# Value projections with 512-wide weights, an earlier split of one weight block, and a copy moved to ScalarE, in a kernel of two transformer blocks

## The chip, the cores and the metric

The kernel runs on one core of a Trainium2 chip. The metric is the device time of one execution in microseconds (us); the median of several executions is compared. All data is float32; many matmuls read a 32-bit format (fp32r) that TensorE streams faster, and each exact product is made of three such matmuls: a weight and an activation are each split into an upper and a lower part, and upper x upper, upper x lower and lower x upper are added up in PSUM.

## The reference

256 tokens of width 1024 pass through two blocks, each with one layer. Cut to what the change touches:

```python
def first_block(x, ...):
    h = rmsnorm(x, g_mix)
    z = h @ w_in                      # columns: pool 512, q 1024, k 1024, v 1024
    v = z[..., 2560:].reshape(B, S, 8, 128)
    y_attn = diff_attention(q, k, v, ...)
    ...                               # pooling branch, gates, output projection, FFN
def second_block(x, ctx, ...):
    hx = modulate(rmsnorm_2(x, ...), sh1, sc1)
    hc = modulate(rmsnorm_2(ctx, ...), csh1, csc1)
    ... nk_c, nv_c = hc @ w_in[kv columns]       # keys and values of 256 context tokens
    ... nq, nk, nv = hx @ w_in                   # queries, keys, values of the tokens
    o_mla = mla_latent_attention(...)
    o_na = neighbourhood_attention(nq, nk, nv, nk_c, nv_c, na_rel_bias)   # 8 heads of 64
    ...                               # output projection, 16 experts in 4 groups, final norm
```

## The kernel before, in words

The program is written for the Tile framework: the Python code emits instructions, Tile allots the buffers, adds the waits and orders the instructions of each engine by priority and by when it reckons them ready. A further dependency without a semaphore can be put between two instructions of one engine with `order(later, earlier)` (line 149); it only fixes their order.

Weights come as blocks of 1 MB, 128 partitions x 2048 columns. `load` (line 179) issues the DMA on the SP queue into one of four raw buffers `w`. `split_block` (line 212) calls `split` (line 188) for each half: ScalarE casts 1024 columns to the upper part (line 192) and VectorE subtracts it for the lower part (line 193), into one of four buffers `whl`. So a block takes two of four, and the next but one block waits for TensorE to be through with it. `mm3` (line 221) issues the three matmuls of one product. `dense_steps` (line 238, matmuls in lines 249 to 251) makes 256 output columns for 256 tokens; its weights are the stationary operand.

In the first block, a planner (`Jobs`, line 93) interleaves generators by rank, with an estimated TensorE cost and a latency at each `yield`. The generators are `feed` (line 710), `stats` (line 490) and two `head_lane`s. `feed` emits two pool blocks (tile upool), then for each pair p of four pairs of heads the query block and the key block (`qk_block`) and the value block (`v_block`), and then eight gate blocks. From the third pair on it waits until both heads of the pair two before are through. `stats` emits the mean of squares of x: `squares` on ScalarE and VectorE (lines 357 to 363, sums in tile sqa), four small matmuls into tile ms (line 369), then on VectorE mse (line 498) and epsq (line 499), then the reciprocal root: logarithm and exponential on ScalarE (tile ry), three operations on VectorE (lines 336 to 338, result rcol). A head waits for its values with `when(("v", p))` (line 677) ahead of the product with the probabilities (tile pv).

The value block is the other way round than `dense_steps`: the activations are stationary and the weights stream. In `v_block` (line 540) each of four blocks streams 256 columns of weights; one PSUM bank holds both halves of the tokens:

```python
for tb in range(2):
    for k in range(8):
        hi, lo = w(k, 256)
        mm3(ps[:, tb * 256:(tb + 1) * 256], (xh[...], xl[...]), (hi, lo), k == 0, k == 7)
```

`scaled_split` (line 318) then empties each half: ScalarE writes vh (line 320), VectorE vl (line 321). Banks 0 and 1 rotate in this stage through `mmbank`: query, value and gate blocks each take the next one; so before, all query blocks were on one bank and all value blocks on the other. Key blocks have bank 2.

In the second block, `feed2` (line 1275) emits the values of the neighbourhood attention (`na_values`, line 954, tile nav) for the context (activations ch, cl) and then for the tokens (hxh, hxl); between them stands the latent projection of the context (`kv_lat`, tile kvl, which has weights of its own, split aside). Both weight blocks are split ahead. The tokens' activations are made meanwhile by `modulated` (line 832). Then come four `na_pair`s (line 981), each with keys (tile nak) and queries (tile naq). Each query, scaled by 0.125, is stored as upper and lower part, twice, on partitions 0 to 63 and 64 to 127, by lines 998 to 1001 in tile napair. The softmax of two lanes of heads follows on VectorE and ScalarE (`softmax_pv`, line 1010: maximum in line 1026, its negation nm in lines 1022 and 1028, exponential in line 1029, transposes tp, casts ph and pl).

The experts come last: 16 experts in turns of four gate and up blocks (tile gu) and two down blocks (tile y), 96 weight blocks of 1 MB through a ring of 17 buffers (`eload`, line 1353, issued in line 1356); a load is issued when its ring buffer is free. TensorE's products there are in line 1754.

Of the kernel before, what the change touches and what calls it, by code (L numbers as in the profile page):

```python
# [15 lines left out]
OP = mybir.AluOpType  # L16
# [6 lines left out]
EPS = 1e-6  # L23
# [34 lines left out]
NAVP = 100  # L58

MM = 0.328  # L60
# [61 lines left out]
def tile_two_blocks(ctx, tc, a):  # L122
    nc = tc.nc
# [17 lines left out]
    def mmbank(name):  # L141
        b = mm_banks[0]
        mm_i[0] += 1
        return bank(b[mm_i[0] % len(b)], name)
# [34 lines left out]
    def load(ap, shape=(128, 2048), slot=None):  # L179
        if slot is None:  # L180
            w = wraw.tile(list(shape), F32, name="w", tag="w")
        else:
            w = big(slot, list(shape), F32, "w")
        with tc.high_priority(offset=0):
            nc.sync.dma_start(w, ap)
        return w

    def split(src, n):
        t = whl.tile([128, 2048], F32R, name="whl", tag="w")
        hi, lo = t[:, 0:n], t[:, 1024:1024 + n]  # L190
        with tc.high_priority(offset=AHEAD_SPLIT):
            nc.scalar.copy(hi, src)  # L192
            nc.vector.tensor_sub(lo, src, hi)  # L193
        return hi, lo

    def split_fine(w):

# [14 lines left out]
    def split_block(w):  # L212
        parts = [split(w[:, i * 1024:(i + 1) * 1024], 1024) for i in range(2)]

        def at(idx, width):
            o = idx * width
            g, r = divmod(o, 1024)
            return parts[g][0][:, r:r + width], parts[g][1][:, r:r + width]
        return at

    def mm3(out, w, x, start, stop):
        i = matmul(out, w[0], x[0], start=start, stop=False).ins
        matmul(out, w[0], x[1], start=False, stop=False)
        matmul(out, w[1], x[0], start=False, stop=stop)
        return i
# [92 lines left out]
    def scaled_split(hi, lo, src, gain):  # L318

        nc.scalar.activation(hi, src, AF.Copy, scale=gain)  # L320
        nc.vector.scalar_tensor_tensor(lo, src, gain, hi, op0=OP.mult, op1=OP.subtract)
# [162 lines left out]
    done = set()  # L484
# [5 lines left out]
    def stats():  # L490

        with low_priority(SQP):
            acc = squares(xT)
        use_table("natural_log_exp_and_others")
        yield 0, LAT_ST
        ms = bank(7, "ms")
        mean_mm(ms, acc)
        nc.vector.tensor_scalar(mse, ms[:, :2], EPS, None, op0=OP.add)
        nc.vector.tensor_scalar(epsq, mse, EPS, None, op0=OP.mult)
        rstd(rcol, mse, 2)  # L500
        yield 0.43, 2.0
        rb_ps = bank(7, "rb_ps")
        rows_of_cols(rb_ps, rcol)
        nc.vector.tensor_copy(rb, rb_ps[:, :T])
        small_inputs()
        yield 0.86, 0.5, when("u")
        for b in range(2):
            nc.vector.tensor_mul(upad[:, 2 * b:2 * b + 2, 16:], ups[b].rearrange("p (m t) -> p m t", m=2),
                                 rb.unsqueeze(1).to_broadcast([128, 2, T]))
        wg = big(11, [128, 2, 512], F32R, "wg")  # L510
        wgh, wgl = wg[:, 0], wg[:, 1]
        copy_split(wgh, wgl, load(a["w_grp"], (128, 512)))
        for g in range(4):
            yield 0, LAT_POOL
            pool_group(g, wgh, wgl)
            yield 0.35
# [22 lines left out]

    def v_block(b):  # L540

        w = split_block(load(a["w_in"][10 + b]))
        ps = mmbank("v")
        for tb in range(2):
            for k in range(8):
                hi, lo = w(k, 256)
                mm3(ps[:, tb * 256:(tb + 1) * 256],
                    (xh[:, k, tb * 128:(tb + 1) * 128], xl[:, k, tb * 128:(tb + 1) * 128]), (hi, lo),
                    k == 0, k == 7)
                yield MM  # L550
        for tb in range(2):
            scaled_split(vh[:, tb, b * 256:(b + 1) * 256], vl[:, tb, b * 256:(b + 1) * 256],
                         ps[:, tb * 256:(tb + 1) * 256], rcol[:, tb:tb + 1])
        done.add(("v", b))

    def gate_block(g):
        half, j = divmod(g, 4)
# [152 lines left out]
    def feed():  # L710
        for b in range(2):
            ups.append(bank(3 + b, "upool"))
            if b == 0:
                yield from dense_steps(ups[b], split_fine(first), xs, groups=[range(i, i + 2) for i in range(0, 8, 2)])
            else:
                yield from dense_steps(ups[b], split_block(load(a["w_in"][b])), xs)
        done.add("u")
        for p in range(4):
            if p >= 2:
                yield 0, 0, lambda: pair[p - 2]["heads"] == 2  # L720
            yield from qk_block(p, 0)
            yield from qk_block(p, 1)
            yield from v_block(p)
            for i in MODQ[p]:
                mod_block(i, MODS.get(i))
        for n, g in enumerate((0, 4, 1, 5, 2, 6, 3, 7)):
            yield from gate_block(g)
            for i in MODG[n]:
                mod_block(i, MODS.get(i))
# [215 lines left out]
    def value_split(t, kb, heads, src):  # L945

        hi, lo = (t[:, kb, heads, n, :] for n in range(2))
        s = src.rearrange("p (h e) -> p h e", e=64)
        copy_split(hi, lo, s)
# [2 lines left out]
    nav = [value_tile(7), value_tile(8)]  # L952

    def na_values():
        wv = [split_block(load(a["w_in2"][4 + b])) for b in range(2)]
        yield
        for n in range(2):
            if n == 1:
                yield "context"
                yield 0, 3.0, when("hx")  # L960
            for b in range(2):
                ps = mmbank("nav")
                for tb in range(2):
                    for k in range(8):
                        mm3(ps[:, tb * 256:(tb + 1) * 256],
                            (srcs[n][0][:, k, tb * 128:(tb + 1) * 128], srcs[n][1][:, k, tb * 128:(tb + 1) * 128]),
                            wv[b](k, 256), k == 0, k == 7)
                        yield MM
                for tb in range(2):
                  with tc.high_priority(offset=NAVP):  # L970
                    value_split(nav[n], tb, slice(4 * b, 4 * b + 4), ps[:, tb * 256:(tb + 1) * 256])

    def proj(ps, w, c0, n, kt=8, width=256, x=None, koff=0):

# [6 lines left out]
    def na_pair(p):  # L981
        w = split_block(load(a["w_in2"][p]))
        nb = load(a["na_bias"][p])
        t = big((3, 6)[p % 2], [128, 2048], F32R, "napair")
        psk = mmbank("nak")
        for n in range(2):
            yield from proj(psk[:, n * 256:(n + 1) * 256], w, 0, n)

        rows = slice(0, 64), slice(64, 128)
        keys = t[:, 0:512], t[:, 512:1024]  # L990
        for j in range(2):
            nc.scalar.copy(keys[j][rows[j]], psk[rows[j]])
            nc.vector.tensor_sub(keys[j][rows[1 - j]], psk[rows[j]], keys[j][rows[j]])
        psq = mmbank("naq")[:, :T]
        yield from proj(psq, w, 128, 1)
        qh, ql = (t[:, 1024:1280], t[:, 1280:1536]), (t[:, 1536:1792], t[:, 1792:2048])
        for j in range(2):
            nc.scalar.activation(qh[j][rows[j]], psq[rows[j]], AF.Copy, scale=0.125)
            nc.vector.scalar_tensor_tensor(ql[j][rows[j]], psq[rows[j]], 0.125, qh[j][rows[j]], op0=OP.mult, op1=OP.subtract)
            nc.scalar.activation(qh[j][rows[1 - j]], psq[rows[j]], AF.Copy, scale=0.125)  # L1000
            nc.vector.scalar_tensor_tensor(ql[j][rows[1 - j]], psq[rows[j]], 0.125, qh[j][rows[j]], op0=OP.mult,
                                           op1=OP.subtract)
        J.add(0, ready(("na", p), 1.2))
        pair["na", p] = qh, ql, keys, nb

# [936 lines left out]
def blocks(w, width):  # L1942
    K, M = w.shape
    return np.ascontiguousarray(
        w.reshape(K // 128, 128, M // width, width).transpose(2, 1, 0, 3).reshape(M // width, 128, -1))


def layout(i):
# [9 lines left out]
    o["cols"] = np.ascontiguousarray(np.concatenate([cols_of(p) for p in parts], axis=1))  # L1958
    o["lambda_qk"] = i["lambda_qk"].reshape(1, 256)
    o["w_in"] = blocks(i["w_in"][0], 256)  # L1960
    o["w_gate"] = blocks(i["w_gate"][0], 256)
    o["w_grp"] = np.ascontiguousarray(i["w_pool_grp"][0].transpose(1, 0, 2).reshape(128, 512))
    o["w_bp"] = blocks(i["w_branch_pool"][0], 512)
# [20 lines left out]
    o["b_mod"] = np.ascontiguousarray(i["b_mod_2"][0].reshape(6, D))  # L1984
    w = i["w_in_2"][0]
    q_lat, na_q, kv_lat, kr, na_k, na_v = np.split(w, np.cumsum([384, 512, 256, 32, 512]), axis=1)
    sw = np.concatenate([kr[:, 16:], kr[:, :16]], axis=1)
    pairs = [p for m in range(4) for p in (na_k[:, m * 128:(m + 1) * 128], na_q[:, m * 128:(m + 1) * 128])]
    o["w_in2"] = blocks(np.concatenate(pairs + [na_v, kv_lat, kr, sw, kr, sw, q_lat[:, 256:], q_lat[:, :256]],
# [63 lines left out]
```

## Time and profile before

| | us |
|---|---|
| median of 3 runs | 875.27 |
| lowest and highest | 875.26, 877.39 |
| the profiled execution | 877.89 |
| its span, first to last instruction | 876.1 |
| TensorE (PE) busy in it | 850.8 |
| VectorE (DVE) busy | 559.7 |
| ScalarE (ACT) busy | 425.9 |

The median is that of executions without the profiler; the profile is of one execution. A row of the order of time has a start, a duration, the engine, the line, the operation and the tiles written and read. Matmuls are pipelined: a row's duration is a modelled one and longer than the distance to the next start, so the cost of a matmul in a queue is read from the starts.

### The profile page before, as it was taken

To read this page: it belongs to the slowest core of one execution; us is meant where nothing else is said; L and a number is where in the kernel's file an instruction comes from. 1 tells how busy PE (TensorE), PEld (TensorE's weight loads), DVE (VectorE), ACT (ScalarE), POOL (GpSimd) and SP (SyncE) were. 2 spreads that over 40 slices of the span, in tenths; PEclk is the share of its full clock that TensorE was granted. 3 is DMA by queue.
4 is the path that set the end of the run, shared out by engine and by line. 5 is a ranking of instruction groups with operands and counts; after the bars stand their busy time and mean duration, and the time that the engine had idled before them with its cause. 6 is when DMAs were issued, how large, how long until landed. Compare 5 with 4: busy or idle time off the path is not lost. (4 is left out here: it accounts for less than half of the span.)

```text
span 876.1 us, 14580 instructions
## 1 busy us (share of the span) xinstructions
PE 850.8 (97%) x5827; PEld 691.9 (79%) x5827; DVE 559.7 (64%) x1137; ACT 425.9 (49%) x800; POOL 15.4 (2%) x28
## 2 busy tenths in 40 slices
PE   8999999999999999999999999999989999999995
PEld 7998999999999999999999988889943333334331
DVE  6898778799988768777855899997741111111104
ACT  6487787744564555546754687797520000000002
POOL 1000000000000000000000000000001000001001
PEclk9999999999999999999999999999899999999998
DMA  7762555577887665768524225546879999999970
GB/s 278 276 246 97 183 177 198 205 266 272 316 300 266 232 251 203 282 206 303 190 78 144 97 79 186 191 144 237 335 263 416 426 427 427 426 426 427 425 315 33
DMA packets 34781, 224.51 MB, mean 256 GB/s; under 512 B 4479, under 2 KB 6143, under 8 KB 8458
## 3 DMA queue, kind: packets, MB, share of 16 engines
q1 hardware_dynamic: 31256, 216.18, 65.3%
q10 hardware_dynamic: 2674, 5.16, 1.6%
q0 software_dynamic: 768, 2.10, 0.6%
q8 instruction: 49, 0.80, 0.4%
q14 instruction: 34, 0.28, 0.1%
HBM read 220.53 MB, written 3.41 MB: 256 GB/s over the span
## 5 line engine op out<-in xcount | busy, mean ns | idle before, releaser
L192 ACT CAST whl<-w 128x1024 fp32r<-128x1024 f32 x155 | 161.9, 1048 | 121.2 <-PE up L251 46.3
L193 DVE TENSOR_TENSOR whl<-w,whl 128x1024 fp32r<-128x1024 f32 x155 | 188.0, 1220 | 42.5 <-ACT whl L192 41.9
L1754 PE MATMUL gu<-w,XG 128*64 128x512 f32 (+1 forms) x512 | 142.7, 603 | 2.5 <-issue 2.5
L1754 PEld LDWEIGHTS gu<-w,XG 128*64 128x64 f32 (+1 forms) x512 | 51.2, 151 | 81.9 <-issue 81.2
L155 ACT ACTIVATE sg<-gu 64x512 f32<-64x512 f32 (+1 forms) x16 | 9.4, 590 | 192.0 <-PE gu L1754 192.0
L896 PE MATMUL dn<-hh,whl 128*128 128x256 f32 x512 | 93.2, 280 | 0.0
L1786 DVE SCALAR_TENSOR_TENSOR h<-sg,small,gu 64x512 f32<-64x512 f32 (+1 forms) x16 | 12.0, 751 | 121.0 <-ACT sg L155 67.5
L406 DVE SCALAR_TENSOR_TENSOR macc<-w,cs,macc 128x512 f32<-128x512 f32 x104 | 74.4, 745 | 9.8 <-DMA w<-w_mod 9.8
L896 PEld LDWEIGHTS dn<-hh,whl 128*128 128x128 f32 x512 | 79.8, 189 | 0.0
L249 PE MATMUL up<-fh,whl 128*128 128x256 f32 x256 | 73.2, 286 | 0.0
L250 PE MATMUL up<-fl,whl 128*128 128x256 f32 x256 | 72.4, 283 | 0.0
L251 PE MATMUL up<-fh,whl 128*128 128x256 f32 x256 | 72.4, 283 | 0.0
L1754 PE MATMUL y<-w,th 128*64 128x512 f32 (+1 forms) x256 | 72.2, 596 | 0.0
L896 PE MATMUL dn<-hl,whl 128*128 128x256 f32 x256 | 72.1, 282 | 0.0
L1754 PEld LDWEIGHTS y<-w,th 128*64 128x64 f32 (+1 forms) x256 | 25.0, 150 | 42.5 <-issue 41.3
L250 PEld LDWEIGHTS up<-fl,whl 128*128 128x128 f32 x256 | 49.1, 192 | 0.1
L251 PEld LDWEIGHTS up<-fh,whl 128*128 128x128 f32 x256 | 49.1, 192 | 0.0
L249 PEld LDWEIGHTS up<-fh,whl 128*128 128x128 f32 x256 | 49.0, 192 | 0.0
L896 PEld LDWEIGHTS dn<-hl,whl 128*128 128x128 f32 x256 | 48.1, 188 | 0.0
L249 PE MATMUL gate<-xh,whl 128*128 128x256 f32 x128 | 36.9, 288 | 0.0
L1797 DVE COPY th<-tpe 128x256 f32<-128x256 f32 (+1 forms) x16 | 7.8, 490 | 45.1 <-PE tpe L1754 45.1
L250 PE MATMUL gate<-xl,whl 128*128 128x256 f32 x128 | 36.3, 283 | 0.0
(515 smaller groups left out, 2123.3 us busy)
## 6 DMA issues: line engine op xcount, KB each, us to landing
w<-e_gate SPq DMA_DIRECT2D x32, 1024.0 KB, 19.6
w<-e_up SPq DMA_DIRECT2D x32, 1024.0 KB, 18.5
w<-e_down SPq DMA_DIRECT2D x32, 1024.0 KB, 19.5
w<-w_mod SPq DMA_DIRECT2D x24, 1024.0 KB, 5.2
w<-w_in SPq DMA_DIRECT2D x22, 1024.0 KB, 5.3
w<-w_up SPq DMA_DIRECT2D x16, 1024.0 KB, 7.0
w<-w_down SPq DMA_DIRECT2D x16, 1024.0 KB, 4.8
w<-w_gate SPq DMA_DIRECT2D x8, 1024.0 KB, 6.2
```

The source lines that it names most:

```text
L155: i = nc.scalar.activation(*args, **kw).ins
L192: nc.scalar.copy(hi, src)
L193: nc.vector.tensor_sub(lo, src, hi)
L249: matmul(o, hi[:, c], x[0], start=n == 0, stop=False, skip_group_check=True)
L250: matmul(o, hi[:, c], x[1], start=False, stop=False, skip_group_check=True)
L251: matmul(o, lo[:, c], x[0], start=False, stop=last, skip_group_check=True)
L406: nc.vector.scalar_tensor_tensor(m, src, c, m, op0=OP.mult, op1=OP.add)
L896: matmul(o, u, v, start=start and n == 0, stop=stop and n == 2, skip_group_check=True)
L1754: i = matmul(*args, **kw).ins
L1786: nc.vector.scalar_tensor_tensor(hs[n][0:m], sg[r], sv[r, g, 4 * g + i:4 * g + i + 1], gu[n][1], op0=OP.mult, op1=OP.mult)
L1797: nc.vector.tensor_copy(hs[n][:, 0:4 * m], tp[:, 0:4 * m])
```

## The change

1. `split` keeps its VectorE instructions in a list, and in `stats` mse (line 498) is ordered behind the first two of them, the lower parts of the second pool block's weights.
2. `v_block` makes 512 columns at a time, for two pairs of heads, from two loads of four k-steps each, into two PSUM banks, one for each half of the tokens. It is emitted after the key blocks of pairs 0 and 2. `na_values` likewise makes 512 columns; each of its weight blocks now holds four k-steps of all columns. The weights are laid out for it on the host.
3. In `na_pair`, the second copy of the queries' lower part is copied by ScalarE from the first, in place of being computed again by VectorE.

```diff
@@ split
             nc.scalar.copy(hi, src)
-            nc.vector.tensor_sub(lo, src, hi)
+            lows.append(nc.vector.tensor_sub(lo, src, hi).ins)
         return hi, lo
+    lows = []
@@ stats
-        nc.vector.tensor_scalar(mse, ms[:, :2], EPS, None, op0=OP.add)
+        summed = nc.vector.tensor_scalar(mse, ms[:, :2], EPS, None, op0=OP.add).ins
+        for i in lows[:2]:
+            order(summed, i)
@@ v_block
-        w = split_block(load(a["w_in"][10 + b]))
-        ps = mmbank("v")
+        pv = [mmbank("v") for _ in range(2)]
+        for kh in range(2):
+            w = split_block(load(a["w_v"][b][:, kh * 2048:(kh + 1) * 2048]))
+            for tb in range(2):
+                for k2 in range(4):
+                    k = 4 * kh + k2
+                    t = slice(tb * 128, (tb + 1) * 128)
+                    mm3(pv[tb], (xh[:, k, t], xl[:, k, t]), w(k2, 512), k == 0, k == 7)
+                    yield 2 * MM
         for tb in range(2):
-            for k in range(8):
-                hi, lo = w(k, 256)
-                mm3(ps[:, tb * 256:(tb + 1) * 256],
-                    (xh[:, k, tb * 128:(tb + 1) * 128], xl[:, k, tb * 128:(tb + 1) * 128]), (hi, lo),
-                    k == 0, k == 7)
-                yield MM
-        for tb in range(2):
-            scaled_split(vh[:, tb, b * 256:(b + 1) * 256], vl[:, tb, b * 256:(b + 1) * 256],
-                         ps[:, tb * 256:(tb + 1) * 256], rcol[:, tb:tb + 1])
-        done.add(("v", b))
+            scaled_split(vh[:, tb, b * 512:(b + 1) * 512], vl[:, tb, b * 512:(b + 1) * 512], pv[tb], rcol[:, tb:tb + 1])
+        done.update((("v", 2 * b), ("v", 2 * b + 1)))
@@ feed
-            yield from v_block(p)
+            if p % 2 == 0:
+                yield from v_block(p // 2)
@@ na_values
-        wv = [split_block(load(a["w_in2"][4 + b])) for b in range(2)]
+        wv = [split_block(load(a["w_nav"][0][:, kh * 2048:(kh + 1) * 2048])) for kh in range(2)]
...
-            for b in range(2):
+            for tb in range(2):
                 ps = mmbank("nav")
-                for tb in range(2):
-                    for k in range(8):
-                        mm3(ps[:, tb * 256:(tb + 1) * 256],
-                            (srcs[n][0][:, k, tb * 128:(tb + 1) * 128], srcs[n][1][:, k, tb * 128:(tb + 1) * 128]),
-                            wv[b](k, 256), k == 0, k == 7)
-                        yield MM
-                for tb in range(2):
-                  with tc.high_priority(offset=NAVP):
-                    value_split(nav[n], tb, slice(4 * b, 4 * b + 4), ps[:, tb * 256:(tb + 1) * 256])
+                t = slice(tb * 128, (tb + 1) * 128)
+                for k in range(8):
+                    mm3(ps, (srcs[n][0][:, k, t], srcs[n][1][:, k, t]), wv[k // 4](k % 4, 512), k == 0, k == 7)
+                    yield 2 * MM
+                with tc.high_priority(offset=NAVP):
+                    value_split(nav[n], tb, slice(0, 8), ps)
@@ na_pair
             nc.scalar.activation(qh[j][rows[1 - j]], psq[rows[j]], AF.Copy, scale=0.125)
-            nc.vector.scalar_tensor_tensor(ql[j][rows[1 - j]], psq[rows[j]], 0.125, qh[j][rows[j]], op0=OP.mult,
-                                           op1=OP.subtract)
+            nc.scalar.copy(ql[j][rows[1 - j]], ql[j][rows[j]])
@@ layout
+    o["w_v"] = blocks(i["w_in"][0][:, 2560:3584], 512)
...
+    o["w_nav"] = blocks(na_v, 512)
```

## Rows read from the trace of the kernel before

**Rows 1.** The page: the span, and section 1, busy time by engine.
```profile
span 876.1 us, 14580 instructions
...
PE 850.8 (97%) x5827; PEld 691.9 (79%) x5827; DVE 559.7 (64%) x1137; ACT 425.9 (49%) x800; POOL 15.4 (2%) x28
```

**Rows 2.** Timeline of TensorE, 17 to 25 us: start us, us, engine, line, operation, tiles.
```profile
17.22 0.28 PE L250 MATMUL upool<-xl,whl 128*128 128x256 f32 x1
18.75 0.38 PE L251 MATMUL upool<-xh,whl 128*128 128x256 f32 x1 [1.25 <-DVE whl L193]
...
24.37 0.28 PE L249 MATMUL q<-xh,whl 128*128 128x256 f32 x1
```

**Rows 3.** Timeline of TensorE, first value block: ten starts, the first and last.
```profile
37.33 0.28 PE L222 MATMUL v<-whl,xh 128*128 128x256 f32 x1
...
38.41 0.28 PE L222 MATMUL v<-whl,xh 128*128 128x256 f32 x1
```

**Rows 4.** Timeline of VectorE, 14.7 to 23 us.
```profile
14.74 0.88 DVE L363 TENSOR_TENSOR sqa<-sqa,sq 128x256 f32<-128x256 f32 x2
17.20 0.16 DVE L498 TENSOR_SCALAR mse<-ms 128x2 f32<-128x2 f32 x1 [1.58 <-PE ms L369]
...
17.47 2.36 DVE L193 TENSOR_TENSOR whl<-w,whl 128x1024 fp32r<-128x1024 f32 x2
...
20.21 2.36 DVE L193 TENSOR_TENSOR whl<-w,whl 128x1024 fp32r<-128x1024 f32 x2
```

**Rows 5.** Timeline of ScalarE, 17 to 20 us.
```profile
17.73 1.99 ACT L192 CAST whl<-w 128x1024 fp32r<-128x1024 f32 x2
```

**Rows 6.** Timeline of TensorE near 544 us: four starts of 512-wide matmuls, first and last.
```profile
544.05 0.39 PE L224 MATMUL vm<-whl,kvn 128*128 128x512 f32 x1
...
544.74 0.39 PE L224 MATMUL vm<-whl,kvn 128*128 128x512 f32 x1
```

**Rows 7.** Timeline of TensorE: last matmul of the first and of the third value block.
```profile
44.73 0.28 PE L224 MATMUL v<-whl,xl 128*128 128x256 f32 x1
...
100.36 0.29 PE L224 MATMUL v<-whl,xl 128*128 128x256 f32 x1
```

**Rows 8.** Timeline of VectorE: the first eviction of those two value blocks.
```profile
46.21 0.48 DVE L321 SCALAR_TENSOR_TENSOR vl<-v,rcol,vh 128x256 fp32r<-128x256 f32 x1
...
105.43 0.48 DVE L321 SCALAR_TENSOR_TENSOR vl<-v,rcol,vh 128x256 fp32r<-128x256 f32 x1
```

**Rows 9.** Instructions of the tile yah, a 512-wide eviction: ns min/median/max, starts.
```profile
L321 DVE SCALAR_TENSOR_TENSOR yal<-tp,gq,yah x4: 742/744/747, 85.1 to 165.0; 128x512 fp32r<-128x512 f32 x4
```

**Rows 10.** Timeline of all engines near 450 us, the tokens' activations in block two.
```profile
449.35 0.69 DVE L325 TENSOR_TENSOR hxl<-modf,hxh 128x512 fp32r<-128x512 f32 x1 [0.31 <-ACT hxh L324]
...
450.10 0.39 PE L224 MATMUL nav<-whl,hxl 128*128 128x256 f32 x1
```

**Rows 11.** Instructions of the tiles napair and oT: ns min/median/max, first and last start.
```profile
L1001 DVE SCALAR_TENSOR_TENSOR napair<-naq,napair x8: 419/422/428, 474.8 to 536.9; 64x256 fp32r<-64x256 f32 x8
...
L324 ACT CAST oT<-os x16: 389/403/409, 504.9 to 617.8; 64x256 fp32r<-64x256 f32 x16
```

**Rows 12.** Waits of TensorE, 465 to 560 us: total us, times, longest.
```profile
PE s L1016 <- DVE mx L1026: 1.1, 2, 0.7
PE vm L222 <- DVE nm L1028: 1.0, 1, 1.0
PE o L1056 <- ACT ph L324: 0.9, 1, 0.9
```

**Rows 13.** Instructions of the experts' weight tiles, 715 to 760 us: their loads.
```profile
DMA to landing us min/median/max: 19.6/19.6/19.6
```

**Rows 14.** Timeline of the SP queue near 710 us.
```profile
710.00 0.33 SPq L1356 DMA_DIRECT2D w<-e_up  x1
```

**Rows 15.** The chain that ended last, 729 to 746 us.
```profile
730.52 13.93 PE gu L1754 x32
```

**Rows 16.** Waits of the SP queue, whole span.
```profile
SPq L1356 <- PE gu L1754: 29.8, 12, 7.3
```

## The prediction

> **What bounds the kernel now.** I read the page first, then the waits, then the order of time on each engine. The page has TensorE busy for 97% of the span [rows 1], and nearly all of it is a queue of short matmuls with no gap: where TensorE saves a matmul or a wait ahead of the experts, what is behind it moves up, as long as nothing else is late there. So the question of each part is what it takes out of TensorE's queue, and what is late next.
>
> The list of waits of TensorE is short. The largest one behind the start and outside the attention heads is early: the matmul of line 250 starts at 17.22 and its successor on line 251 at 18.75 [rows 2], where the step in this queue is 0.12 [rows 3]. The releaser is the lower part of a weight block. VectorE, which makes it, stood idle: its last sum of squares ended at 14.74 + 0.88 = 15.62, it then waited 1.58 for the mean's matmul, and only behind mse and epsq came the two lower parts, in 2.36 [rows 4]. That is a queue's order, not a lack of time.
>
> **Part one, the lower parts ahead of mse.** TensorE's loss there is 18.75 - (17.22 + 0.12) = 1.41. With the order turned, the lower parts run from 15.62, the first is done at 16.80 and the second at 17.98; the first is needed at 17.34, so the whole wait goes: **-1.41**. What it costs: mse is ready from 17.98 instead of 17.20, 0.78 later. Behind the logarithm that waits for it on ScalarE stand two casts for the first query block, at 17.73 for 1.99 [rows 5]; they end at 20.50 instead of 19.72. Their lower parts started at 20.21 and took 2.36 [rows 4]; they can start once the first cast is done, near 19.5, and end near 21.9, against a first query matmul at 24.37 [rows 2], now 22.96. About 1 us of cover remains, so I cost this at nothing; if it is gone, up to 0.78 comes back. The gain lies between 0.63 and 1.41.
>
> **Part two, value projections of the first block.** 192 matmuls of 256 columns become 96 of 512. Nine starts of the narrow kind lie 1.08 apart (37.33 to 38.41), 0.12 each [rows 3]; three of the wide kind lie 0.69 apart (544.05 to 544.74), 0.23 each [rows 6]. 192 x 0.12 - 96 x 0.23 = 23.04 - 22.08: **-0.96**, all on TensorE's queue.
> The Trainium skill (TensorE: Matmul & The Clock Gate, "Wait — 56ns, not 53.3ns?") speaks against that: a stream of matmuls costs its columns plus a fixed 2.5 ns, so only 0.24 would be saved here, and the sum would be smaller by 0.72 in each of the two blocks. The two steps are measured in this kernel, so the sum goes by them.
> The loads are the same number of megabytes, in another order on the SP queue, and each still waits for its buffer. Evictions fall from eight to four on each engine, off the path.
>
> What is added is a wait. A block of values now fills both rotating banks, so the next query block writes the bank of the first token half, which ScalarE and VectorE must have emptied. It is complete 12 x 0.23 = 2.76 before TensorE is through with the other half: that is the cover. Before, the first value block's last matmul ended at 44.73 + 0.28 = 45.01 and the third one's at 100.36 + 0.29 = 100.65 [rows 7]; VectorE was done with the first half at 46.69 and at 105.91 [rows 8], 1.68 and 5.26 later. A 512-wide eviction takes 0.744 on VectorE [rows 9] instead of 0.48; with as much more on ScalarE, add 0.54: 2.2 and 5.8. The wait is 0 at the nearer place of the first block and 5.80 - 2.76 = 3.04 at the second. The late one stood behind four modulation multiplies, which in the new code are emitted after the whole block, while its bank is complete 2.76 earlier; so I lean to the low end: **+0.5** for both places together, with 0 and 3.0 (6.1, if both are late) kept for the range.
> Pair 1's and pair 3's queries and keys now come 48 x (0.23 - 0.12) = 5.3 later. Pair 1 is covered by pair 0's heads, which feed TensorE meanwhile; pair 3 by eight gate blocks of 48 x 0.12 = 5.8 each behind it. If that cover is gone, what is left of 5.3 shows.
>
> **Part three, value projections of the second block.** The same arithmetic gives 0.96, half for the context and half for the tokens. The context half runs while the tokens' activations are still being made: their first lower part ends at 449.35 + 0.69 = 450.04 and TensorE's matmul on it starts at 450.10 [rows 10]. TensorE's other work there just reaches; a shorter filler may only wait longer. The token half behind it counts in full. I take **-0.7**, between 0.48 and 0.96. The context needs the second weight block after 2.8 of work instead of 5.8; the other context work in this queue stands by to fill that, so nothing is added.
>
> **Part four, the queries' copy.** Eight VectorE operations of 0.422 go, eight ScalarE copies come; the nearest of that shape, SBUF to SBUF, took 0.403 [rows 11]. VectorE loses 3.4 us, ScalarE gains 3.2. What TensorE can get from it is in its waits between 465 and 560: 1.1 and 1.0 behind VectorE's maxima and 0.9 behind ScalarE [rows 12]. The bounds: all of VectorE's 2.1 gained; or the copies stand ahead of the exponentials in three of four pairs, 3 x 0.8 = 2.4 lost. The 1.1 fell in one head while a pair's queries were being made, where one such operation (0.42) goes from VectorE's queue just ahead: **-0.45**.
>
> **The sum.** -1.41 - 0.96 + 0.5 - 0.7 - 0.45 = -3.02. The profiled execution took 877.89 (span 876.1 [rows 1], and 1.8 around it), 2.6 over the median of 875.27; I subtract from either alike: 874.9 for that execution, **872.3** as a median. About 0.3%, 2.6 us, is what a measurement can tell from no change here; the forecast lies just beyond it.
>
> **The rivals.**
> - One late bank: the fourth query block waits the whole 3.04. Then -0.48, **874.8**, chance 0.13. For it: the 5.26 above. Against: those multiplies move.
> - The experts' weights hold the end. Their loads land 19.6 after issue [rows 13]; the second block of the ninth turn, issued at 710.00 [rows 14], lands at 729.6, and the turn, at 730.52 with 32 matmuls in 13.93 [rows 15], needs it at about 730.96. If this stream does not start earlier too, only 1.36 of the gain arrives: **873.9**, chance 0.07. Against: the SP queue waited 29.8 in 12 places for gate and up matmuls [rows 16], so the stream moves up with TensorE.
> - Width brings nothing: with two steps of 0.12 for a wide matmul, parts two and three lose 0.96 + 0.7, **873.9**, chance 0.03. The skill's rule above points there; [rows 3, 6] speak against it.
> - The order does not do what it says, because another instruction takes VectorE's place: without part one -1.61, **873.7**, chance 0.06.
> - Slower: both places where a query block follows a value block wait 3.04, 6.1 in place of 0.5, and the copies return part four: -3.02 + 5.6 + 0.45 = +3.0, **878.3**, chance 0.11. It decides from 3.5 us of such waits on. Against: the first place has 2.2 against a cover of 2.76.
> - More: no bank wait, all of part three, and 2.1 from part four: -5.4, **869.8**, chance 0.05.
> The forecast has 0.55, its own range being 870.3 to 873.0.
>
> **The numbers.** Faster: 0.51 of the forecast's 0.55 and the last rival, 0.56. Same: the remaining 0.04 and the rivals at 874.8, 873.9, 873.9 and 873.7, 0.33. Slower: 0.11. The range goes from the last rival to between one late bank and two: 869.5 to 876.6.
>
> **What would show it.** Right: no wait of TensorE near 17, the first pair's query block about 1.4 earlier; 512-wide value matmuls 0.23 apart; the query blocks after them starting with a gap under 0.6; the context keys of the second block 3 earlier; the first expert turn 3 earlier and no wait for weights in it. Wrong: a gap of TensorE on a query block released by the values' lower part; a later exponential with the copies before it; an expert matmul released by a DMA.

## The result, and the profile after

The changed kernel takes 871.82 us (median of 20 runs, 868.44 to 876.97), the kernel before, run beside it, 877.31 (20 runs): ratio 0.995, 95% interval 0.9931 to 0.9968. By the ratio that is 4.4 us less, between 2.8 and 6.1; the two medians alone lie 5.5 apart. One of the 20 runs before, at 934.75, was slow and is not in the ratio. In a later set the pair gave 871.19 and 876.55, ratio 0.9929 (0.99 to 0.9958).

The profiled execution of the changed kernel took 869.78. Its page, the span and section 1:
```profile
span 867.8 us, 14178 instructions
...
PE 844.0 (97%) x5635; PEld 675.3 (78%) x5635; DVE 555.9 (64%) x1121; ACT 427.5 (49%) x800; POOL 15.3 (2%) x28
```
The span is 8.3 shorter than in [rows 1], nearly twice what the ratio says. Two single executions can't be set against each other as wholes, so I cut both into stages at the same matmuls. The view by windows, first of the kernel before, then of the changed one: stretch, its length, busy time (and instructions) of PE, PEld, DVE, ACT and POOL, PE's granted clock (1.00 is 2.4 GHz, 0.50 is 1.2 GHz), DMA share, GB/s. The stretches are: first query matmul to last gate matmul; values of block two; first neighbourhood key to last modulation matmul; from there to the last output matmul; from there to the routing's position matmuls.
```profile
24.40:181.10 156.70, 153.02 (x1264) 147.61 (x1263) 126.14 (x301) 113.33 (x268) 0.10 (x1) 1.00 0.55 194
424.20:462.90 38.70, 38.28 (x310) 37.23 (x310) 27.87 (x53) 22.37 (x42) 0.00 (x0) 1.00 0.39 137
462.90:551.00 88.10, 84.97 (x650) 80.53 (x650) 71.44 (x171) 58.48 (x120) 0.00 (x0) 1.00 0.38 128
551.00:621.10 70.10, 68.60 (x482) 61.46 (x480) 57.45 (x126) 54.98 (x109) 0.00 (x0) 1.00 0.60 223
621.10:630.30 9.20, 9.20 (x68) 9.20 (x66) 7.22 (x24) 6.99 (x26) 0.00 (x0) 0.75 0.89 338
```
```profile
20.90:174.80 153.90, 151.58 (x1167) 141.50 (x1166) 126.17 (x296) 111.29 (x264) 0.10 (x1) 1.00 0.56 197
418.00:455.50 37.50, 36.88 (x214) 31.92 (x214) 27.61 (x49) 22.48 (x39) 0.00 (x0) 1.00 0.38 140
455.50:541.40 85.90, 84.85 (x653) 80.43 (x652) 67.13 (x163) 60.78 (x127) 0.00 (x0) 1.00 0.39 131
541.40:614.90 73.50, 72.38 (x509) 64.33 (x507) 60.98 (x130) 57.25 (x117) 0.00 (x0) 1.00 0.59 217
614.90:621.80 6.90, 4.49 (x40) 4.09 (x38) 4.54 (x19) 4.67 (x17) 0.00 (x0) 1.00 0.94 353
```
Read down the second column: -2.8, -1.2, -2.2, then **+3.4**, then -2.3. The stretch from 181 to 424 takes 243 in both, the experts 221.9 in both. The fourth row is a surprise: 27 more matmuls in it, and 3.4 longer. The fifth row of the kernel before has the clock at 0.75, which belongs to that execution (below). Most of the rest of the 8.3 is the start: the mean's matmul ms starts at 16.7 before and at 13.9 after, and from there to the first query matmul 0.7 is saved.

All the kernels run, cut in this way from their profiles, one execution each (us; "ms" is a start, the others are lengths; N is from the first neighbourhood key to the last position matmul, the sum of the three columns after "values 2"; the clock is that of the last of these three; the ratio is that of the times to the kernel before, with its interval):
```
kernel          ms   ms-Q  Q-gate values2 heads  output routing     N  clock  ratio
before         16.7   7.7   156.7   38.7   88.1   70.1    9.3   167.5  0.75
changed        13.9   7.0   153.9   37.5   85.9   73.5    6.9   166.3  1.00  0.995  (.9931-.9968)
after_again    16.7   6.2   156.8   37.4   85.9   73.5    6.9   166.3  1.00  0.9929 (.99-.9958)
e1_order       14.4   6.8   156.6   38.6   88.4   70.1    7.4   165.9  1.00  0.9983 (.9953-1.0012)
e2_v512        17.4   7.7   153.8   38.7   88.1   70.1    7.6   165.8  1.00  0.9986 (.9957-1.0014)
e3_nav512      16.3   7.7   159.1   37.5   88.1   70.0    7.4   165.5  1.00  0.9973 (.9947-.9999)
e4_copy        14.5   7.7   156.2   38.7   85.9   73.8    6.9   166.6  1.00  1.0024 (.9998-1.0051)
m1_moved       14.8   9.3   158.5   38.7   88.1   70.1    7.3   165.5  1.00  0.9986 (.9962-1.0011)
c4_behind      13.8   7.8   156.7   38.6   85.9   70.1    9.3   165.3  0.76  0.999  (.9965-1.0016)
f_no4          16.3   6.2   154.3   37.4   88.0   70.1    7.9   166.0  0.90  0.9926 (.9898-.9955)
f_no4_again    15.2   6.8   153.8   37.5   88.0   70.0    7.4   165.4  1.00  0.9937 (.9911-.9962)
g1_behind      14.8   6.9   154.8   37.5   85.8   70.1    8.5   164.4  0.84  0.9896 (.9864-.9928)
g1_again       15.3   6.8   154.0   37.5   85.8   70.1    7.4   163.3  1.00  0.9895 (.9856-.9933)
g2_filled      15.8   6.3   154.0   37.5   85.8   70.1    8.1   164.0  1.00  0.9873 (.9837-.991)
```
Parts one to three each move one column and leave the others within 0.3, apart from the clock (the routing, 9.3 in m1_moved, 158.5 and 159.1 in "Q-gate", 156.8 in after_again, all taken up below); part four moves three. That is what makes effects of 1 us readable here, where the intervals of the times are 5 us wide.

### The profile page after: what moved, and what is told of

It reads as the page before. It is cut to its first block, busy times and chain, and to the rows that moved or that the text cites. A ratio compares the mean times of both kernels' runs of the same rounds, so it can differ in the third digit from the quotient of the medians.

```text
span 867.8 us, 14178 instructions
## 1 busy us (share of the span) xinstructions
PE 844.0 (97%) x5635; PEld 675.3 (78%) x5635; DVE 555.9 (64%) x1121; ACT 427.5 (49%) x800; POOL 15.3 (2%) x28
```

## The experiments

**Each part alone.** Part one (e1_order):
```diff
+        for i in lows[:2]:
+            order(summed, i)
```


> Part one alone: the first two lower parts ahead of mse, all else as before. Theory (a queue's order costs TensorE one wait): no wait of 1.25 between the matmuls of the first sums' weight block near 17; from the mean's matmul ms to the first query matmul 6.3 to 6.9 us instead of 7.72 (24.37 - 16.65), since the cast on ScalarE may still hold up to 0.6; nothing else moves, first query block to last gate matmul stays 156.8 within 1. Time ratio 0.9984 to 0.999. Rival (the 3.4 by which the changed kernel reaches its first query block earlier are all this part's): that block starts at 20.9 and the ratio is 0.996.

Measured: 6.8, from 7.7. The rival's start is nearly met too (21.2), but the kernel with part four alone, whose start is as before, has its ms at 14.5 as well and needs 7.7 from there. Why 0.4 of wait is left is seen in the changed kernel, where it is 0.47, timelines of TensorE and of VectorE (to be held against [rows 2, 4]), and of ScalarE:
```profile
14.58 0.28 PE L253 MATMUL upool<-xl,whl 128*128 128x256 f32 x1
15.32 0.39 PE L254 MATMUL upool<-xh,whl 128*128 128x256 f32 x1 [0.47 <-DVE whl L193]
```
```profile
12.91 0.88 DVE L366 TENSOR_TENSOR sqa<-sqa,sq 128x256 f32<-128x256 f32 x2
14.04 2.36 DVE L193 TENSOR_TENSOR whl<-w,whl 128x1024 fp32r<-128x1024 f32 x2 [0.25 <-ACT whl L192]
16.32 0.15 DVE L501 TENSOR_SCALAR mse<-ms 128x2 f32<-128x2 f32 x1
```
```profile
12.96 2.00 ACT L192 CAST whl<-w 128x1024 fp32r<-128x1024 f32 x2 [0.60 <-DMA w<-w_in]
```
VectorE now makes the lower parts ahead of mse, as ordered, but in this execution TensorE came early, and the weights' load and ScalarE's cast are late next. Where TensorE came late (f_no4, ms at 16.3) nothing is left of the wait; TensorE and VectorE there:
```profile
16.88 0.28 PE L253 MATMUL upool<-xl,whl 128*128 128x256 f32 x1
17.00 0.28 PE L254 MATMUL upool<-xh,whl 128*128 128x256 f32 x1
```
```profile
14.62 0.88 DVE L366 TENSOR_TENSOR sqa<-sqa,sq 128x256 f32<-128x256 f32 x2
15.41 2.35 DVE L193 TENSOR_TENSOR whl<-w,whl 128x1024 fp32r<-128x1024 f32 x2
17.68 0.15 DVE L501 TENSOR_SCALAR mse<-ms 128x2 f32<-128x2 f32 x1
```
Over the eight kernels with part one the stage took 6.2 to 7.0, against 7.7 or 7.8 in five of the six without it (in m1_moved, 9.3, the clock fell from 18.3 to 21.7): 0.7 to 1.5 gained.

Part two (e2_v512):
```diff
-            yield from v_block(p)
+            if p % 2 == 0:
+                yield from v_block(p // 2)
```
with the 512-wide `v_block` and its weights.

> Part two alone: value projections of the first block 512 wide. Theory after seeing the changed kernel: the stage from the first query matmul to the last gate matmul falls from 156.8 to 154.1 (0.96 by width, the rest from waits in the attention heads that other matmuls now fill), no query block waits for its bank, the start and everything behind 181 as before; ratio 0.997. Rival one (the prediction's term): 0.96 by width less 0.5 for a bank, so 156.3; ratio 0.9995. Rival two (the 1.7 of head waits is not this part's but drift between executions): 155.8; ratio 0.9989.

Measured: 153.8. The stage gained 2.9, six times the prediction's 0.46; no query block waited. The time's interval holds all three figures.

To see whether the order or the width did it, the narrow blocks were put where the wide ones stand (m1_moved):
```diff
-            yield from v_block(p)
+            if p % 2 == 0:
+                yield from v_block(p)
+                yield from v_block(p + 1)
```


> The move in part two without the width: both value blocks of a pair of pairs one after the other, still 256 columns wide in the old layout. The stage from the first query matmul to the last gate matmul took 156.7 before, 153.8 with part two alone, 153.9 in the changed kernel. Theory (1.9 of those 2.9 come from head waits that fall elsewhere once the value blocks stand together, 0.96 from width): 154.8; ratio 0.998. Rival (all of it comes from the width, since a shorter value block moves everything behind it): 156.7, ratio 1.

Measured: 158.5; about 1.7 of that is a fall of the clock behind a wait of 1.13 (0.79 between 120 and 128, so 0.21 x 8), and without it the stage is where it was before. So my theory fell: standing together brings nothing. One thing does change with the move: when the loads come. Waits of VectorE in this stage for the modulation weights, of the kernel before and then of m1_moved (total, times, longest):
```profile
DVE macc L406 <- DMA w<-w_mod: 4.3, 3, 2.3
```
```profile
DVE macc L406 <- DMA w<-w_mod: 0.4, 1, 0.4
```
In the kernel with part two alone this wait is 0.7 in one place, in the changed one 0.6, but 2.9 in another execution of it (after_again). In the kernel before, this is what stood behind the longest of the waits, timelines of VectorE and TensorE:
```profile
153.51 1.42 DVE L406 SCALAR_TENSOR_TENSOR macc<-w,cs,macc 128x512 f32<-128x512 f32 x2 [2.28 <-DMA w<-w_mod]
154.84 0.55 DVE L325 TENSOR_TENSOR al<-tp,ah 128x384 fp32r<-128x384 f32 x1
```
```profile
154.09 0.28 PE L223 MATMUL pv<-vl,ah 128*128 128x128 f32 x1
155.45 0.33 PE L224 MATMUL pv<-vh,al 128*128 128x128 f32 x1 [1.07 <-DVE al L325]
```
A modulation multiply that nobody is in a hurry for waits first in VectorE's queue for its weights; the attention's lower part `al` is behind it, and TensorE behind that. In the five kernels that have the value blocks where they were (e4_copy, e1_order, before, c4_behind, e3_nav512) the longest of these waits was 1.7, 2.1, 2.3, 2.3 and 3.1, and TensorE's wait behind `al` 0.5, 0.9, 1.1, 1.1 and 1.9. The issue of that load on the SP queue, in the kernel before, with part two alone and in m1_moved:
```profile
146.68 0.33 SPq L185 DMA_DIRECT2D w<-w_mod  x1
```
```profile
141.93 0.33 SPq L185 DMA_DIRECT2D w<-w_mod  x1
```
```profile
144.43 0.33 SPq L185 DMA_DIRECT2D w<-w_mod  x1
```
VectorE came to its multiply 4.6 behind the issue in the kernel before (153.51 less the 2.28 of wait), where the load took 6.8 to land, and 7.5 and 8.4 behind it in the other two (at 149.38 and 152.81), without a wait. So the move brings this load in time, with narrow matmuls as with wide ones. But it does not make the stage shorter by itself: m1_moved has new waits of TensorE, 1.13 for a sum of squares and 0.91 for a cast of ScalarE. With part two alone, too, TensorE waits about as long nearby, for something else:
```profile
154.68 0.33 PE L222 MATMUL pv<-vh,ah 128*128 128x128 f32 x1 [1.10 <-ACT sbias L683]
```
TensorE's idle time in the stage (its length less the busy time in the view by windows) is 3.7 before, 2.3 with part two alone and 3.3 in m1_moved. So of the 2.9, 0.96 is the width and 1.4 is less idle time, of which the move alone shows 0.4; 0.5 I can't place. What takes out the other 1.0 of idle time, and why the old order has that load late, stays open.

Part three (e3_nav512):
```diff
-        wv = [split_block(load(a["w_in2"][4 + b])) for b in range(2)]
+        wv = [split_block(load(a["w_nav"][0][:, kh * 2048:(kh + 1) * 2048])) for kh in range(2)]
```
with the loops that go with it.

> Part three alone: value projections of the second block 512 wide. Theory: from the first context value matmul to the first neighbourhood key matmul 37.5 to 38.0 us instead of 38.7 (0.7 to 1.2 saved); the neighbourhood stage behind it (first key matmul to last modulation matmul) stays at 88.1 within 0.5; ratio 0.9988. Rival: moving that stage ahead also takes the 2.2 out of it that the changed kernel shows (88.1 to 85.9); then 3 in all, ratio 0.9965.

Measured: 37.5, and the stage behind unmoved at 88.1. The rival falls. (The 159.1 of the stage ahead belongs to a longer wait for a load and to the clock, below: the instructions there are those of the kernel before, in the same order.)

Part four (e4_copy):
```diff
-            nc.vector.scalar_tensor_tensor(ql[j][rows[1 - j]], psq[rows[j]], 0.125, qh[j][rows[j]], op0=OP.mult,
-                                           op1=OP.subtract)
+            nc.scalar.copy(ql[j][rows[1 - j]], ql[j][rows[j]])
```


> Part four alone: the queries' second lower half copied by ScalarE. Theory after seeing the changed kernel: the neighbourhood stage (first key matmul to last modulation matmul) falls from 88.1 to about 86 because waits of TensorE behind VectorE's maxima go (3.1 idle to about 1); ratio 0.9976. Rival one (the prediction's term): 87.6, ratio 0.9995. Rival two (copies stand ahead of exponentials): up to 90.5, ratio 1.0027.

Measured: the heads' stage fell to 85.9, as the theory had it, and yet the time did not fall: 1.0024, with 1 inside its interval. The give-back is in the next column: 73.8 for 70.1. Waits of TensorE in the changed kernel from 455.5 to 622, total, times, longest:
```profile
PE pos L1517 <- DVE ohr L1499: 1.8, 1, 1.8
...
PE xps L1447 <- DVE x2T L1442: 0.6, 1, 0.6
PE o L1057 <- ACT ph L327: 0.5, 1, 0.5
...
```
Both waits behind VectorE of [rows 12] are gone, 2.1 in all, the bound I had named, and of the third 0.5 is left of 0.9; a wait of 0.4 behind ScalarE's writing of napair is new. In their place TensorE waits in the routing, behind x2T and ohr. Its timeline there shows why:
```profile
612.65 0.97 PE L1456 MATMUL lg<-route,x2T 128*128 128x20 f32 x8
613.47 0.36 PE L1379 MATMUL wo<-oT,whl 128*128 128x256 f32 x1
...
615.72 0.33 PE L1447 MATMUL xps<-ident,x2T 128*128 128x128 f32 x1 [0.58 <-DVE x2T L1442]
...
621.43 0.27 PE L1517 MATMUL pos<-ohr,before 128*128 128x8 f32 x1 [1.83 <-DVE ohr L1499]
```
Twelve transposes (xps) and 16 logits (lg) now stand ahead of the last twelve output matmuls (wo); before, all wo stood ahead of all of them. The order of each engine's instructions is fixed when the program is built, and with another engine mix it came out otherwise. The code ties the transposes to the output matmul that is emitted last, `m = 7`; `m = 4` and 5, in another bank, were scheduled behind that one. The routing's chain (the last x2T, xps, a sum of squares on ScalarE, ohr) begins with the last wo, so putting these ahead delays it, and the fillers made for its wait run out.

**Part four undone, and the order held.** f_no4 has the VectorE instruction back:
```diff
-            nc.scalar.copy(ql[j][rows[1 - j]], ql[j][rows[j]])
+            nc.vector.scalar_tensor_tensor(ql[j][rows[1 - j]], psq[rows[j]], 0.125, qh[j][rows[j]], op0=OP.mult, op1=OP.subtract)
```


> The changed kernel with part four undone (VectorE copies the queries' lower half, as before). Stage N is the time from the first neighbourhood key matmul to the last position matmul of the routing: 165.7, 165.8 and 165.5 in the kernels with part one, two or three alone, 166.6 with part four alone, 166.3 in the changed kernel. Theory (part four saves 2.2 of waits in the neighbourhood heads and gives back 3 behind them, because transposes and logits then stand ahead of twelve matmuls of the output projection): N 165.5 here with the waits behind VectorE back, the transposes of the routing behind all output matmuls again; 0.8 faster than the changed kernel, ratio to before 0.9945. Rival (part four is worth its 0.45 or more): N 166.8 or more, ratio 0.9965.

g1_behind keeps the copy and orders transposes and first logits behind all eight of the last products (c4_behind is the same edit on the kernel with part four alone):
```diff
-        for m in range(8):
-            product = mixed_tile(3, m)[1]
+        products = [mixed_tile(3, m)[1] for m in range(8)]
...
-                    order(turned, product)
+                    for last in products:
+                        order(turned, last)
...
```


> The changed kernel, with the transposes and first logits of the routing ordered behind all eight last output matmuls instead of behind the last one emitted. Theory: the 2.2 saved in the heads is kept; the last output matmul ends 156.3 after the first key matmul (159.4 in the changed kernel), and 7.0 later the position matmuls start, so N falls from 166.3 to 163.4; ratio to before 0.992. Rival one (the order of these matmuls doesn't matter, since the chain behind the heads sets the end): N stays 166.3, ratio 0.995. Rival two (the transposes' earlier start is what saved time, so undoing it costs): N 167.

> Part four alone, with the same order for transposes and logits held. Theory: N 163.5 instead of 166.6 with part four alone and 165.7 without it; ratio to before 0.9975, where part four alone gave 1.0024. Rival (the copies on ScalarE themselves cost the heads or what is behind them): N 166 or more, ratio 1.001 or more.

Measured: "output" is back at 70.1 in both, while "heads" stays at 85.8 and 85.9. N is 164.4 in g1_behind, 1.0 above its theory, with the clock at 0.84 in the routing; its ratio, 0.9896, is better than the theory's 0.992; c4_behind has 165.3 and 0.999, which alone decides nothing: its clock fell in the routing, 1.9 of the 9.3. f_no4 has 166.0 with a smaller fall of the clock.

So the three were run again, or anew, on one chip:

> The changed kernel once more, on one chip with the two versions that differ from it in the routing. Theory (stage N, first neighbourhood key matmul to last position matmul, is 166.3 here, 165.5 to 166.0 without part four and 163.4 to 164.4 with part four and the order held): ratio to before 0.995, slowest of these four. Part one: the remaining wait at the lower part is 0 to 0.5, shorter the later the mean's matmul starts (0 at 16.3, 0.47 at 13.9 so far). No query block waits for the bank that a value block left. Rival (the spread between chips made the difference): all four within 0.2 per cent.

> Part four undone, once more beside the changed kernel. Theory: N 165.5 to 166, 0.3 to 0.8 us faster than the changed kernel (ratio to before 0.994). Rival (part four is worth its 2.2, and what stands behind is drift): 2 us slower than the changed kernel, 0.997.

> Transposes and logits ordered behind all output matmuls, once more beside the changed kernel. Theory: N 163.4, or 164.4 where TensorE's granted clock falls in the routing; 2 to 3 us faster than the changed kernel, ratio to before 0.992. Rival: the same as the changed kernel, 0.995.

Measured, medians: the changed kernel 871.19, part four undone 871.28, order held 867.58. The rival of the spread between chips falls. Part four is worth nothing as it stands (N 166.3 with it, 165.4 without); with the order held it is worth 2.1 by N and 3.7 by the medians. The windows of heads, output and routing, and the routing's timeline of TensorE, in g1_again:
```profile
456.70:542.50 85.80, 84.74 (x652) 80.38 (x651) 67.07 (x163) 60.68 (x127) 0.00 (x0) 1.00 0.38 131
542.50:612.60 70.10, 68.97 (x479) 61.16 (x478) 59.62 (x128) 55.43 (x109) 0.00 (x0) 1.00 0.61 224
612.60:620.00 7.40, 7.40 (x68) 7.26 (x66) 5.88 (x20) 6.29 (x25) 0.00 (x0) 1.00 0.92 347
```
```profile
612.60 0.28 PE L1381 MATMUL wo<-oT,whl 128*128 128x256 f32 x1
...
612.75 1.98 PE L1447 MATMUL xps<-ident,x2T 128*128 128x128 f32 x16
614.57 3.65 PE L1457 MATMUL lg<-route,x2T 128*128 128x20 f32 x32
618.06 1.72 PE L173 MATMUL fill<-before,ones_r 128*128 128x256 f32 x13
619.68 0.27 PE L1519 MATMUL pos<-ohr,before 128*128 128x8 f32 x1
```
N is 163.3, where 163.4 was expected, 3.0 under the changed kernel's, and the wait for ohr is gone. The last edit puts fillers among the narrow logits (g2_filled):
```diff
-IDLE = (13, 7)
+IDLE = (11, 7)
...
+            if m in (2, 4, 6):
+                turned = idle(2, fill, logit)
```


> As the last one, with three pairs of filler matmuls between the routing's 32 narrow logit matmuls and two fewer behind them. In four profiles so far the granted clock stood at its lower level behind the logits and the position matmuls came 1 to 2 us later. Theory (the narrow matmuls are what the clock falls on, and wider ones among them hold it): N 163.4 with no fall of the clock in the stage from the last output matmul to the position matmuls; ratio 0.991. Rival (the fall comes from elsewhere, and the fillers only lengthen TensorE's queue): N 164.4 or more with the clock at 0.75 to 0.85 in that stage, ratio 0.993.

Measured: clock 1.00, N 164.0, so the fillers cost 0.7 against a g1_again whose clock did not fall either. Median 865.84 against 867.58, whose intervals overlap. One execution doesn't show that the fillers hold the clock; that stays open. Against the kernel before, the two versions are faster by about 1.0% and 1.3%; their medians lie 3.6 and 5.4 under the changed kernel's 871.19 of the same set.

## Why the prediction was right, and where it was not

Direction and size held: -3.02 was forecast, -4.4 came, and 871.82 is in the range. Part of the closeness is luck: the base I took, 875.27, lay 2.0 under the median of all 20 runs, and the sum was 1.4 short by the ratio, 2.5 by the medians; the two errors nearly cancel. Of the terms only the width came as sized; the others missed in both directions.

- **Part one**, -1.41: the mechanism was right, the size 0.7 to 1.5. That the whole wait goes was read off one execution, in which TensorE came late; where it came early, the cast took over. The bound of 0.63 was the better guess for such an execution.
- **Part two, width**: -0.96 held. In the changed kernel, first value block, timeline of TensorE, five starts, the first and the last:
```profile
34.14 0.40 PE L226 MATMUL v<-whl,xh 128*128 128x512 f32 x1
...
35.07 0.39 PE L227 MATMUL v<-whl,xl 128*128 128x512 f32 x1
```
  0.93 for four steps is 0.23 each, as in [rows 6]. The rival without a gain by width falls. The Trainium skill (TensorE: Matmul & The Clock Gate, "Wait — 56ns, not 53.3ns?") has a fixed 2.5 ns beside the columns, by which the steps would be 0.109 and 0.216, as estimates from that page; the trace differs at both widths, 0.12 and 0.23.
- **Part two, bank wait**, +0.5: it was 0 at both places. Timeline of TensorE where the query block follows the value block, at the first and second place, and VectorE's evictions of the first half:
```profile
47.63 0.40 PE L227 MATMUL v<-whl,xl 128*128 128x512 f32 x1
47.86 0.28 PE L252 MATMUL q<-xh,whl 128*128 128x256 f32 x1
...
101.32 0.40 PE L227 MATMUL v<-whl,xl 128*128 128x512 f32 x1
101.55 0.28 PE L252 MATMUL q<-xh,whl 128*128 128x256 f32 x1
```
```profile
44.76 0.75 DVE L324 SCALAR_TENSOR_TENSOR vl<-v,rcol,vh 128x512 fp32r<-128x512 f32 x1
...
98.86 0.75 DVE L324 SCALAR_TENSOR_TENSOR vl<-v,rcol,vh 128x512 fp32r<-128x512 f32 x1
```
  The bank is empty at 45.51 and 99.61, needed at 47.86 and 101.55: about 2 us of margin at both. The rivals with one and with two late banks fall. The 5.26 of before, behind four modulation multiplies, did not come again.
- **Part two, the step that failed**: "The loads are the same number of megabytes, in another order on the SP queue, and each still waits for its buffer." I took another order for no cost and no gain, and so the sum has no term for TensorE's waits in this stage. The stage gained 2.9: beside the 0.96 of the width, TensorE was idle for 1.4 less, and 0.5 is not placed. The order did matter to VectorE, whose 4.3 of waits for modulation weights, in the profile of before, I had not read: they fell to 0.7, and TensorE's 1.07 behind the longest is gone. But this is not shown to be the gain, since m1_moved has the loads in time as well, and its stage is not shorter. Why the wide blocks leave TensorE less idle stays open.
- **Part three**, -0.7: 1.2. The context half was not swallowed (25.6 to 25.3), and the token half gave 0.8; together more than the 0.96 of the arithmetic, the rest not resolved.
- **Part four**, -0.45: net 0.9 the other way by N (166.3 against 165.4), nothing by the times. Bounds and mechanism in the heads were right (2.1 gone, the upper bound); the step that failed is "What TensorE can get from it is in its waits between 465 and 560". The part that gave it back lies behind 560, and not by exponentials behind copies, but by the order that the build chose.
- **The experts' weights**: 221.9 us from the first gate and up matmul to the last down matmul in both, and no wait of TensorE for a load in the changed kernel. The stream moved up with TensorE, as the prediction argued.

## What to carry to other kernels

Cut the profiles of both kernels at the same instructions and compare stages; the span of one execution against another can be off by the size of what you look for. An edit that saves a wait can cost an order further on: after any change of engine look again at where the scheduler put the next dependent chain, and tie that chain to all of its producers, not to the one that is emitted last. Before costing a moved load at nothing, read the waits of the engine that consumes it, and what is queued behind that wait; and when such a wait is gone, look at the length of the stage before calling it the gain, since another wait may stand in its place.

## What the runs showed of the hardware

**A longer wait, and a slower clock behind it.** In e3_nav512, VectorE, the same instructions as before:
```profile
154.01 1.41 DVE L406 SCALAR_TENSOR_TENSOR macc<-w,cs,macc 128x512 f32<-128x512 f32 x2 [3.10 <-DMA w<-w_mod]
```
and TensorE:
```profile
155.94 0.33 PE L224 MATMUL pv<-vh,al 128*128 128x128 f32 x1 [1.89 <-DVE al L325]
...
157.85 0.42 PE L251 MATMUL gate<-xh,whl 128*128 128x256 f32 x1
158.07 0.42 PE L249 MATMUL gate<-xh,whl 128*128 128x256 f32 x1
```
The load took 7.65 to land where it had taken 6.83 in the kernel before, TensorE waited 1.89 in place of 1.07, and from 157.6 to 161.1 its steps were 0.21 in place of 0.12, the lower level of the granted clock, some 1.5 us on top. In after_again VectorE waited 2.9 for a modulation load; waits of TensorE of 1.07 and 0.95 near 136 were followed by a clock of 0.79 between 136 and 144, and its stage took 156.8 in place of 153.9. m1_moved's fall came behind a wait of 1.13. The wait of 1.07 in the kernel before and the 1.10 of e2_v512 were not followed by one, so what decides it is not shown.

**The same order of instructions, another clock.** The routing ran at 1.00 in ten of these profiles and at 0.75 to 0.90 in four, 0.5 to 2 us longer, whatever the kernel (before, f_no4, g1_behind, c4_behind; f_no4 and f_no4_again are one program). At the start of the experts the clock fell in eleven, which took 221.7 to 222.1 from the first gate and up matmul to the last down matmul, and not in three (e2_v512, g1_again, g2_filled), which took 220.2.

**The start is not the same each time.** In kernels whose start is identical (before, parts two, three and four alone) the mean's matmul starts at 16.7, 17.4, 16.3 and 14.5; TensorE's granted clock rises from 0.50 to 1.00, and its steps fall from 0.21 to 0.12, at 14.7, 15.8, 14.3 and 11.3; in the first three it had waited 0.65, 1.10 and 0.34 for a weight cast near 10, in the last for none. The changed kernel had its ms at 13.9 in one execution and at 16.7 in the other. This is where 2.8 of the 8.3 in the spans came from.
